# A two-layer decoder trunk on one core: side-by-side products in every later sub-layer, one PSUM pair for the retention's values, paired squares at the start, and no adaLN work in a sub-layer's first three tiles

## The chip, the core and the metric

The kernel runs on one core of a Trainium2 chip. A core has TensorE (PE in the profile, with PEld for its weight loads), VectorE (DVE), ScalarE (ACT), GpSimd (POOL) and SyncE (SP), which here only issues transfers. The metric is the device time of one execution in microseconds (us).

## What is computed

A sequence of 256 positions with 1024 features goes through two layers of three sub-layers each: a SwiGLU feed-forward block (FFN), a mixer (retention in layer 0, a short convolution in layer 1), and a second FFN. Each sub-layer is normalized and modulated by a conditioning vector (adaLN):

```
mod = (silu(c) @ ada_w[l] + ada_b[l])          # shift, scale, gate of the three sub-layers
h = rmsnorm(x, g) * (1 + scale) + shift
x = x + 0.5 * gate * ((silu(h @ w_gate) * (h @ w_up)) @ w_out)      # FFN, 2816 wide
x = x + gate * retention(h)      # q, k, v, g = h @ w_in; 4 heads; (silu(g) * rmsnorm(o)) @ w_out
x = x + gate * short_conv(h)     # b, c, u = h @ w_in; (b * conv3(c * u)) @ w_out
```

All inputs are float32, and the result keeps float32 accuracy.

## The kernel before

Activations lie with 128 features on the partitions and the 256 positions along the row, so x is eight parts x[k]. Every float32 value v is split into two float32r halves, hi and lo = v - hi, and a product of weights W and activations h is the sum of three: W_hi h_hi, W_hi h_lo and W_lo h_hi. `product` issues them for one 128 x 128 weight block in one of two forms. In the *plain* form (lines 287 to 289) there are three matmuls. In the *side-by-side* form (line 285), used where the PSUM region is twice as wide as the operand, one matmul of 512 columns makes W_hi h_hi and W_hi h_lo in two halves of a PSUM bank, and a second (line 289, 256 columns) adds W_lo h_hi to the first half; the halves are added on the way out.

A *tile* of weights is 2048 columns (1 MB, 16 blocks), that is two output blocks of 128 features. `prepare` splits a raw tile: hi by a copy on ScalarE (line 245), lo by a subtraction on VectorE or, for a part of the tiles, on GpSimd (line 250). The pools hold five raw tiles, six hi halves and six lo halves. The list `jobs` fixes the order of the weight tiles; `weights` keeps up to four loaded ahead.

The operand comes in two forms. The *biased* operand `h` is x * scale, split, with the adaLN shift in two further columns (258 in all); it needs no norm, so a sub-layer can begin on it before the norm is known, and `normalized` (line 325) multiplies the product by the reciprocal norm `r` afterwards. The *whole* operand, built by `whole` (lines 433 to 444), is the finished normalized and modulated input: x * r (line 437, alternately VectorE and GpSimd), scale and shift on ScalarE (line 438), the hi copy on ScalarE (line 331) and lo on VectorE (line 332), for each of eight parts, through three rotating buffers `xr`. Before the change only the retention builds it. There the first three tiles (`BIASED`) are plain on the biased operand, and the tiles after them use the whole one: the first of those goes part by part over k and can begin before all parts are there, q and k and v are plain, and the last five gates are side by side, evicted in `projected` by a ScalarE copy of one half (line 312) and a VectorE addition (line 313). The FFNs after the first, and the convolution, run all their input tiles plain on the biased operand. The output projections of all sub-layers are side by side already.

PSUM is four pairs of banks; from the first FFN on, one pair holds the broadcast conditioning vector for good, which leaves three. AdaLN vectors are made by VectorE: a 1 MB tile of `ada_w` is loaded into a raw buffer and reduced by two instructions (line 120). `pace` decides after each weight tile whether a further adaLN tile is loaded (at most one) and reduces the one loaded earlier; it keeps away only from the border between a sub-layer's input and output tiles.

In the retention, step by step, one head's values are projected, then `normalize` of the head before last and `values` of the last one follow: eight matmuls into two pairs of banks, four squares, and a sum of squares by a matmul with ones (line 358). At the program's start the sum of squares of x is eight such matmuls, ahead of everything. Engines run their own instructions in order; a scheduler wrote that order.

## Time and profile before

| what | value |
|---|---|
| median of 3 runs | 1095.13 us (1094.88 to 1095.41) |
| the profiled execution | 1094.71 us, span of its instructions 1092.9 us |
| TensorE busy | 1067.8 us (98% of the span) |
| VectorE, ScalarE, GpSimd busy | 830.8, 578.0, 391.0 us (76%, 53%, 36%) |
| mean granted clock of TensorE | 0.997 of 2.4 GHz |

Matmuls are pipelined, so TensorE's busy time doesn't tell whether it runs at its best: the distance between the starts of matmuls does. About 1.8 us of the time lie around the span.

### The profile page before, as it was taken

The page shows a single profiled execution, that of the slowest core. Times are in us where ns is not written, and L with a number is a line of the kernel's source. Part 1 is how long each engine was busy: PE and PEld are TensorE (multiplying, and loading weights), DVE is VectorE, ACT ScalarE, POOL GpSimd, SP SyncE. Part 2 cuts the span into 40 slices and gives each one's busy share as a digit, 9 for nine tenths or more (in the row PEclk, how much of TensorE's full clock was granted, in tenths as well). Part 3 has the DMA queues.
Part 4 walks back from the last instruction along what each step waited for, and adds up shares of the span by engine and source line. Part 5 has one row for each costly group of instructions (what it writes and reads, how often), then busy time and mean ns, then how long its engine had stood idle before and what let it go on. Part 6 is the DMA issues. An engine that isn't in the chain of part 4 may idle for free.

```text
span 1092.9 us, 19439 instructions
## 1 busy us (share of the span) xinstructions
PE 1067.8 (98%) x7706; PEld 1008.9 (92%) x7706; DVE 830.8 (76%) x1089; ACT 578.0 (53%) x923; POOL 391.0 (36%) x339
## 2 busy tenths in 40 slices
PE   8999999999998999999999999999999989999996
PEld 7999988999887889999988999998899989999985
DVE  6999776998558898887678878767798686666454
ACT  4364444663367655545555644545564484454442
POOL 0034355345354432332445133344411442323352
PEclk9999999999999999999999999999999999999998
DMA  9977779867555687777679767767885545553441
GB/s 344 364 275 275 295 280 314 314 239 296 208 221 198 227 308 274 268 277 261 219 267 324 300 249 297 266 223 264 305 317 210 190 156 191 173 188 123 156 133 39
DMA packets 44573, 268.51 MB, mean 246 GB/s; under 512 B 4801, under 2 KB 6977, under 8 KB 19906
## 3 DMA queue, kind: packets, MB, share of 16 engines
q1 hardware_dynamic: 43138, 266.56, 67.1%
q8 instruction: 60, 0.98, 0.4%
q10 hardware_dynamic: 1344, 0.71, 0.2%
q14 instruction: 31, 0.25, 0.1%
HBM read 266.20 MB, written 1.05 MB: 245 GB/s over the span
## 4 chain that ended last, share of the span: by engine, by line
PE 59%; DVE 2%; issue 0%; ACT 0%; DVEq 0%; ACTq 0%
PE ps L289 20%; PE ps L288 14%; PE ps L287 14%; PE ps L285 11%; DVE lo L250 1%; PE ps L358 0%; DVE rsum L511 0%; DVE h L412 0%; DVE raw L804 0%; DVE r L800 0%; DVE x L514 0%; ACT hi L245 0%; DVEq L877 0%; DVE x L516 0%; ACT std L370 0%
## 5 line engine op out<-in xcount | busy, mean ns | idle before, releaser
L250 DVE TENSOR_TENSOR lo<-raw,hi 128x1024 fp32r<-128x1024 f32 (+1 forms) x300 | 366.6, 1230 | 176.6 <-ACT hi L245 161.1
L245 ACT CAST hi<-raw 128x1024 fp32r<-128x1024 f32 (+2 forms) x408 | 377.7, 937 | 221.2 <-PE ps L288 123.3
L288 PE MATMUL ps<-h,hi 128*128 128x258 f32 (+1 forms) x1520 | 430.4, 283 | 1.7 <-DVE h L412 1.5
L287 PE MATMUL ps<-h,hi 128*128 128x258 f32 (+1 forms) x1520 | 430.5, 283 | 1.1 <-DVE sum L325 1.1
L289 PE MATMUL ps<-h,lo 128*128 128x258 f32 (+1 forms) x1520 | 430.5, 283 | 0.0
L250 POOL TENSOR_TENSOR lo<-raw,hi 128x384 fp32r<-128x384 f32 (+1 forms) x108 | 201.5, 1867 | 290.4 <-ACT hi L245 290.0
L288 PEld LDWEIGHTS ps<-h,hi 128*128 128x128 f32 x1520 | 288.7, 190 | 2.6 <-DVE h L412 1.3
L287 PEld LDWEIGHTS ps<-h,hi 128*128 128x128 f32 x1520 | 289.0, 190 | 1.8 <-ACT sg L586 0.7
L289 PEld LDWEIGHTS ps<-h,lo 128*128 128x128 f32 x1520 | 288.7, 190 | 0.0
L285 PE MATMUL ps<-act,hi 128*128 128x512 f32 x616 | 217.5, 398 | 0.6 <-DVE rsum L511 0.6
L289 PE MATMUL ps<-act,lo 128*128 128x256 f32 x704 | 197.8, 281 | 0.0
L332 POOL TENSOR_TENSOR act<-av,act 128x256 fp32r<-128x256 f32 x88 | 84.0, 957 | 251.2 <-ACT act L331 242.8
L120 DVE CUSTOM_DVE_ANT_0 raw<-raw,ps,misc 128x1024 f32<-128x1024 f32 x124 | 154.5, 1274 | 0.0
L285 PEld LDWEIGHTS ps<-act,hi 128*128 128x128 f32 x616 | 115.6, 188 | 29.4 <-DVE rsum L511 1.7
L289 PEld LDWEIGHTS ps<-act,lo 128*128 128x128 f32 x704 | 133.1, 189 | 0.3 <-DVE lo L250 0.3
L331 ACT CAST act<-av 128x256 fp32r<-128x256 f32 x88 | 35.5, 405 | 100.4 <-DVE av L590 78.3
L325 DVE TENSOR_TENSOR sum<-ps,r 128x516 f32<-128x516 f32 (+1 forms) x103 | 70.7, 690 | 16.1 <-PE ps L289 15.8
L590 DVE SCALAR_TENSOR_TENSOR av<-sum,sg 128x256 f32<-128x256 f32 x66 | 51.9, 786 | 17.8 <-ACT sg L589 17.8
L289 PE MATMUL ps<-whole,lo 128*128 128x256 f32 x208 | 58.5, 281 | 0.0
L589 ACT ACTIVATE sg<-sum 128x256 f32<-128x256 f32 x66 | 33.6, 509 | 26.3 <-DVE sum L325 25.9
L341 ACT ACTIVATE sq<-x 128x256 f32<-128x256 f32 x48 | 19.7, 416 | 51.6 <-DVE x L514 44.3
L348 POOL TENSOR_TENSOR acc<-acc,sq 128x256 f32<-128x256 f32 x32 | 28.0, 875 | 38.8 <-ACT sq L341 33.7
(132 smaller groups left out, 1296.2 us busy)
## 6 DMA issues: line engine op xcount, KB each, us to landing
raw<-in_ffn_in SPq DMA_DIRECT2D x80, 1024.0 KB, 4.9
raw<-in_ada_w SPq DMA_DIRECT2D x64, 1024.0 KB, 5.5
raw<-in_ffn_out SPq DMA_DIRECT2D x64, 704.0 KB, 4.2
raw<-in_ada_w SPq DMA_DIRECT2D x16, 512.0 KB, 6.8
raw<-in_ffn_in SPq DMA_DIRECT2D x16, 512.0 KB, 7.6
raw<-in_ret_g SPq DMA_DIRECT2D x8, 1024.0 KB, 5.1
raw<-in_ret_qk SPq DMA_DIRECT2D x8, 1024.0 KB, 5.1
raw<-in_ret_v SPq DMA_DIRECT2D x8, 1024.0 KB, 4.8
```

The source lines that it names most:

```text
L120: ins = nc.vector.tensor_tensor_reduce(out=w, in0=w, in1=state["cond"], scale=1.0, scalar=misc[:, C_ADAB + 72 * l + col:C_ADAB + 72 * l + ...
L245: nc.scalar.copy(out=hi, in_=raw[:, c:c + m])
L250: eng.tensor_tensor(out=lo, in0=raw, in1=hi, op=ALU.subtract)
L285: nc.tensor.matmul(out=ps, lhsT=hi, rhs=m.rearrange("p n s -> p (n s)"), start=start, stop=False)
L287: nc.tensor.matmul(out=ps, lhsT=hi, rhs=m[:, 0], start=start, stop=False)
L288: nc.tensor.matmul(out=ps, lhsT=hi, rhs=m[:, 1], start=False, stop=False)
L289: nc.tensor.matmul(out=ps[:, :n], lhsT=lo, rhs=m[:, 0], start=False, stop=stop)
L325: nc.vector.tensor_tensor(out=y[:, :, :n], in0=ps[:, :, :n], in1=r[:, :n].unsqueeze(1).to_broadcast([P, 2, n]), op=ALU.mult)
L331: hi = nc.scalar.copy(out=dst[:, 0], in_=src)
L332: lo = eng.tensor_tensor(out=dst[:, 1], in0=src, in1=dst[:, 0].bitcast(F32), op=ALU.subtract)
L589: nc.scalar.activation(out=sg, in_=y[:, 0, :S], func=AF.Silu, bias=y[:, 0, S:S + 1])
L590: nc.vector.scalar_tensor_tensor(out=av, in0=y[:, 1, :S], scalar=y[:, 1, S:S + 1], in1=sg, op0=ALU.add, op1=ALU.mult)
```

## The change

Every sub-layer after the first now builds the whole operand and, after three biased tiles, uses the side-by-side form for its inputs: the three later FFNs (19 of 22 tiles each) and the convolution (9 of 12). For that the pool of 2 KB slots grows from 22 to 30; the conditioning vector moves from a buffer of its own into one of the six of the hi halves, until it is copied to PSUM in the first FFN, and the scaled x of the first sub-layer moves into slots. `values` writes all four blocks of a head into one pair of banks and runs ahead of `normalize`. The squares of x are added in pairs before the sum by matmul. `pace` also does nothing in a sub-layer's first three tiles.

```diff
-    slot_p = ctx.enter_context(tc.tile_pool(name="slot", bufs=22))
+    slot_p = ctx.enter_context(tc.tile_pool(name="slot", bufs=30))
...
-    cond = const.tile([P, D], F32, name="cond")
+    cond = whi_p.tile([P, D], F32, name="cond", tag="hi")
...
-        if any(o - BEFORE <= n < o + BEHIND for o in outputs):
+        if any(o - BEFORE <= n < o + BEHIND for o in outputs) or any(b <= n < b + BIASED for b in begins):
             return
         reduce_loaded()
...
             if f == 1:
+                begins.append(len(jobs))
                 if l % 2 == 0:
...
+            begins.append(len(jobs))
             jobs += [(a["ffn_in"][l, f, b], 2048) for b in range(FB)]
...
-            for i, pair in enumerate(x_pairs):
-                sq = tmp.tile([P, 2, S], F32, name="sq2", tag="rot" if i % 2 else "sum")
-                (nc.gpsimd if i == 1 else nc.vector).tensor_tensor(out=sq, in0=pair, in1=pair, op=ALU.mult)
-                total([sq[:, 0, :], sq[:, 1, :]], ps, i == 0, i == KB // 2 - 1)
+            for i in range(2):
+                sqs = []
+                for j, eng in ((2 * i, nc.vector), (2 * i + 1, nc.gpsimd)):
+                    sq = tmp.tile([P, 2, S], F32, name=f"sq{j}", tag="rot" if i else "sum")
+                    eng.tensor_tensor(out=sq, in0=x_pairs[j], in1=x_pairs[j], op=ALU.mult)
+                    sqs.append(sq)
+                (nc.gpsimd if i else nc.vector).tensor_tensor(out=sqs[0], in0=sqs[0], in1=sqs[1], op=ALU.add)
+                total([sqs[0][:, 0, :], sqs[0][:, 1, :]], ps, i == 0, i == 1)
...
-        for ps in first_projections(h) if n == 0 else [begun]:
-            activate(ps)
+        if n == 0:
+            for ps in first_projections(h):
+                activate(normalized(ps, r, S), None)
+        else:
+            src["whole"] = whole(n, src["r"])
         while len(act) < FB:
-            activate(projections(h))
+            if n:
+                activate(*projected(src))
+            else:
+                activate(normalized(projections(h), r, S), None)
...
             blocks = []
+            ps = banks()
+            for b in range(4):
+                c = slice(b * P, (b + 1) * P)
+                o = ps[:, b // 2, b % 2 * S:(b % 2 + 1) * S]
+                nc.tensor.matmul(out=o, lhsT=v[hd][0][:, c], rhs=sc[:, :S], start=True, stop=False)
+                nc.tensor.matmul(out=o[:, P:], lhsT=v[hd][1][:, c], rhs=sc[:, S:S + P], start=False, stop=True)
             for half in range(2):
-                ps = banks()
...
+            if 0 <= step - 1 < HEADS:
+                raw_o[step - 1] = values(step - 1, sc[step - 1])
             if 0 <= step - 2 < HEADS:
                 o[step - 2] = normalize(step - 2, *raw_o[step - 2])
-            if 0 <= step - 1 < HEADS:
-                raw_o[step - 1] = values(step - 1, sc[step - 1])
...
-    def short_conv(n, h, r, begun):
+    def short_conv(n, src):
         gated = []
+        src["whole"] = whole(n, src["r"])
...
-            taps(d, normalized(projections(h) if d else begun, r), convs[d])
+            taps(*projected(src), convs[d])
```

On TensorE, at the third sub-layer's fourth input tile (its first on the whole operand), two of the eight parts stood as follows before; `h0` and `h1` are parts of the biased operand, `hi` and `lo` the weight halves:

```order
L287 MATMUL ps_4751<-h0_4369,hi_4533 128x258
L288 MATMUL ps_4751<-h0_4369,hi_4533 128x258
L289 MATMUL ps_4751<-h0_4369,lo_4534 128x258
L287 MATMUL ps_4751<-h1_4374,hi_4533 128x258
L288 MATMUL ps_4751<-h1_4374,hi_4533 128x258
L289 MATMUL ps_4751<-h1_4374,lo_4534 128x258
```

And now, one part after the other for both output blocks:

```order
L288 MATMUL ps_4785<-whole_4595,hi_4527 128x512
L292 MATMUL ps_4785<-whole_4595,lo_4528 128x256
L288 MATMUL ps_4785<-whole_4595,hi_4531 128x512
L292 MATMUL ps_4785<-whole_4595,lo_4532 128x256
L288 MATMUL ps_4785<-whole_4601,hi_4527 128x512
L292 MATMUL ps_4785<-whole_4601,lo_4528 128x256
```

Three matmuls of 258 columns became two, of 512 and 256, for each block, and the first such tile needs the parts one by one.

On VectorE, at the start of the same sub-layer, the reciprocal of the norm was followed by this (`ps_986` is the conditioning vector in PSUM, line 120 the adaLN reduction, `av` the FFN's product of gate and up):

```order
L376 RECIPROCAL r_4599<-std_4595 128x256
L250 TENSOR_TENSOR lo_4538<-raw_4531,hi_4537 128x1024
L120 ISA raw_4469,mod1_96<-raw_4469,ps_986,misc_79 128x1024
L120 ISA mod1_96 128x1
L120 ISA raw_4469,mod1_96<-raw_4469,ps_986,misc_79 128x1024
L120 ISA mod1_96 128x1
L325 TENSOR_TENSOR sum_4602<-ps_4530,r_4599 128x2x258
L250 TENSOR_TENSOR lo_4615<-raw_4612,hi_4614 128x1024
L590 SCALAR_TENSOR_TENSOR av_4605<-sum_4602,sg_4604 128x256
```

Now it is followed by this:

```order
L379 RECIPROCAL r_4589<-std_4585 128x256
L253 TENSOR_TENSOR lo_4532<-raw_4525,hi_4531 128x1024
L440 TENSOR_TENSOR xr_4592<-x0_91,r_4589 128x256
L440 TENSOR_TENSOR xr_4604<-x1_92,r_4589 128x256
L328 TENSOR_TENSOR sum_4640<-ps_4524,r_4589 128x2x258
L253 TENSOR_TENSOR lo_4653<-raw_4650,hi_4652 128x1024
L335 TENSOR_TENSOR whole_4595<-xr_4592,whole_4595 128x256
L335 TENSOR_TENSOR whole_4601<-xr_4598,whole_4601 128x256
L335 TENSOR_TENSOR whole_4607<-xr_4604,whole_4607 128x256
L440 TENSOR_TENSOR xr_4616<-x2_93,r_4589 128x256
L594 SCALAR_TENSOR_TENSOR av_4643<-sum_4640,sg_4642 128x256
L328 TENSOR_TENSOR sum_4708<-ps_4649,r_4589 128x2x258
```

The adaLN reductions left this place, and the building of the whole operand came between the weight splits and the evictions.

On TensorE, in the retention's third step, the sum of squares of head 0 (`acc`) stood ahead of the values of head 1 (`sc`, `v`), four matmuls to each of two PSUM tiles (two of each four are shown); the first and the last row belong to the projections of two heads' values:

```order
L658 MATMUL ps_3446<-hi_3348,whole_2547 128x512
L358 MATMUL ps_3523<-acc_3444,ones_82 128x256
L691 MATMUL ps_3534<-sc_3322,v_3414 128x256
L692 MATMUL ps_3534<-sc_3322,v_3416 128x128
...
L691 MATMUL ps_3541<-sc_3322,v_3414 128x256
L692 MATMUL ps_3541<-sc_3322,v_3416 128x128
...
L656 MATMUL ps_3578<-hi_3380,whole_2505 128x512
```

Now the values come first, and all eight (two are shown) go into one PSUM tile:

```order
L668 MATMUL ps_3443<-hi_3346,whole_2543 128x512
L701 MATMUL ps_3520<-sc_3320,v_3412 128x256
L702 MATMUL ps_3520<-sc_3320,v_3414 128x128
...
L361 MATMUL ps_3547<-acc_3441,ones_82 128x256
L666 MATMUL ps_3574<-hi_3378,whole_2501 128x512
```

One PSUM tile less is taken in a step, and the sum of squares moved behind the eight matmuls.

## Rows read from the trace of the kernel before

**Rows 1.** The page of the profiled execution: busy time and instructions of two engines, and the chain of work that ended last by engine.

```profile
PE 1067.8 (98%) x7706; PEld 1008.9 (92%) x7706; DVE 830.8 (76%) x1089; ACT 578.0 (53%) x923; POOL 391.0 (36%) x339
...
PE 59%; DVE 2%; issue 0%; ACT 0%; DVEq 0%; ACTq 0%
```

**Rows 2.** TensorE's `lo` product (line 289) alone, of which there is one for each 128 x 128 weight block, in seven stretches: the input projections of the third, fourth, fifth and sixth sub-layer from their second tile on, then one gate tile of the retention, five output tiles of the retention, and seven half output columns of the fourth sub-layer. Columns: the stretch and its length in us, busy us (instructions that touch the stretch), granted clock (1.00 is 2.4 GHz), DMA share, GB/s. Of the last three counts one instruction began before the stretch.

```profile
419.32:541.58 122.26, 95.76 (x336) 1.00 0.72 267
609.89:732.71 122.82, 95.10 (x336) 1.00 0.71 261
800.99:865.12 64.13, 50.08 (x176) 1.00 0.65 234
897.50:1019.21 121.71, 94.84 (x336) 1.00 0.50 172
356.75:362.30 5.55, 4.43 (x17) 1.00 0.35 106
375.12:402.86 27.74, 22.17 (x81) 1.00 0.71 249
561.68:588.89 27.21, 21.62 (x78) 1.00 0.88 305
```

**Rows 3.** Busy us (instructions) of PE, PEld, DVE, ACT and POOL in the input projections of the third and the sixth sub-layer, in this order after the length.

```profile
419.32:541.58 122.26, 122.26 (x1010) 122.23 (x1009) 97.38 (x123) 62.81 (x95) 39.27 (x34) 1.00 0.72 267
...
897.50:1019.21 121.71, 121.71 (x1011) 121.68 (x1010) 76.19 (x77) 60.32 (x87) 34.38 (x30) 1.00 0.50 172
```

**Rows 4.** Timeline (start us, duration us, engine, line) at the start of the retention: TensorE at its first tile on the whole operand, then VectorE around it.

```profile
228.43 0.28 PE L289 MATMUL ps<-whole,lo 128*128 128x256 f32 x1
229.81 0.39 PE L287 MATMUL ps<-whole,hi 128*128 128x256 f32 x1 [1.10 <-ACT whole L331]
231.10 0.39 PE L288 MATMUL ps<-whole,hi 128*128 128x256 f32 x1 [0.90 <-DVE whole L332]
...
215.19 1.74 DVE L376 RECIPROCAL r<-std 128x256 f32<-128x256 f32 x1
...
222.79 1.27 DVE L120 CUSTOM_DVE_ANT_0 raw<-raw,ps,misc 128x1024 f32<-128x1024 f32 x1
223.99 1.27 DVE L120 CUSTOM_DVE_ANT_0 raw<-raw,ps,misc 128x1024 f32<-128x1024 f32 x1
...
230.63 0.76 DVE L332 TENSOR_TENSOR whole<-xr,whole 128x256 fp32r<-128x256 f32 x2
```

**Rows 5.** Groups of instructions (count, busy us, mean ns of one, idle us before) of VectorE and GpSimd between 205 and 235 us: those that build the whole operand.

```profile
L332 DVE TENSOR_TENSOR whole<-xr,whole 128x256 fp32r<-128x256 f32 x8 | 4.6, 615 | 0.0
L437 DVE TENSOR_TENSOR xr<-x,r 128x256 f32<-128x256 f32 x4 | 2.1, 550 | 0.0
...
L437 POOL TENSOR_TENSOR xr<-x,r 128x256 f32<-128x256 f32 x4 | 4.1, 1030 | 12.1 <-DVE r L376 8.2 <-DVE whole L332 3.9
```

**Rows 6.** Timeline of TensorE in the retention's values, gates and sums of squares; in brackets the idle time before an instruction and what ended it.

```profile
314.92 0.38 PE L692 MATMUL ps<-sc,v 128*128 128x128 f32 x2
316.49 0.70 PE L691 MATMUL ps<-sc,v 128*128 128x256 f32 x2 [1.18 <-ACT std L370]
...
330.33 0.38 PE L692 MATMUL ps<-sc,v 128*128 128x128 f32 x2
331.69 0.70 PE L691 MATMUL ps<-sc,v 128*128 128x256 f32 x2 [0.98 <-ACT std L370]
...
343.78 0.50 PE L285 MATMUL ps<-whole,hi 128*128 128x512 f32 x1 [1.91 <-DVE sum L313]
...
350.67 0.70 PE L358 MATMUL ps<-acc,ones 128*128 128x256 f32 x2 [0.97 <-POOL acc L348]
```

**Rows 7.** Timeline at the start of the third sub-layer: VectorE, then GpSimd; and VectorE at the start of the fifth.

```profile
412.94 0.41 DVE L348 TENSOR_TENSOR acc<-acc,sq 128x256 f32<-128x256 f32 x1
415.52 2.40 DVE L348 TENSOR_TENSOR acc<-acc,sq 128x256 f32<-128x256 f32 x1 [1.38 <-ACT sq L341]
...
421.02 1.75 DVE L376 RECIPROCAL r<-std 128x256 f32<-128x256 f32 x1
...
415.25 2.39 POOL L250 TENSOR_TENSOR lo<-raw,hi 128x1024 fp32r<-128x1024 f32 x1 [6.72 <-ACT hi L245]
...
803.37 1.75 DVE L376 RECIPROCAL r<-std 128x256 f32<-128x256 f32 x1
```

**Rows 8.** Groups of VectorE in the third sub-layer's input projections (420 to 541 us), then of ScalarE and VectorE in the retention's side-by-side gates (340 to 372 us).

```profile
L250 DVE TENSOR_TENSOR lo<-raw,hi 128x1024 fp32r<-128x1024 f32 x35 | 44.9, 1284 | 18.7 <-ACT hi L245 18.7
L120 DVE CUSTOM_DVE_ANT_0 raw<-raw,ps,misc 128x1024 f32<-128x1024 f32 x22 | 27.3, 1277 | 0.0
L325 DVE TENSOR_TENSOR sum<-ps,r 128x516 f32<-128x516 f32 x21 | 14.5, 692 | 2.2 <-PE ps L289 2.2
L590 DVE SCALAR_TENSOR_TENSOR av<-sum,sg 128x256 f32<-128x256 f32 x21 | 13.7, 652 | 4.5 <-ACT sg L589 4.5
...
L312 ACT COPY sum<-ps 128x512 f32<-128x512 f32 x5 | 2.9, 579 | 0.0
...
L313 DVE TENSOR_TENSOR sum<-ps,sum 128x512 f32<-128x512 f32 x5 | 3.3, 669 | 0.0
```

**Rows 9.** Timeline at the program's start: TensorE's sums of squares, and GpSimd's square of one pair of x.

```profile
8.23 4.23 PE L358 MATMUL ps<-sq,ones 128*128 128x256 f32 x12
...
6.36 1.04 POOL L476 TENSOR_TENSOR sq<-x 128x512 f32<-128x512 f32 x1 [5.39 <-DMA x<-in_x]
```

More of the change, by code (lines that the diff above doesn't have):

```diff
@@ L201, in trunk_kernel @@
     outputs = []
+    begins = []
     ready = {}
@@ L483, in first_modulated @@
                 if k % 2 == 0:
-                    pair = tmp.tile([P, 2, S], F32, name=f"xs{k}", bufs=1)
+                    pair = in_halves(slot(F32, "xs"))
                 xs = pair[:, k % 2, :]
@@ L686, in values @@
             blocks = []
-            for half in range(2):
-                ps = banks()
-                for i in range(2):
-                    c = slice((2 * half + i) * P, (2 * half + i + 1) * P)
-                    nc.tensor.matmul(out=ps[:, i, :S], lhsT=v[hd][0][:, c], rhs=sc[:, :S], start=True, stop=False)
-                    nc.tensor.matmul(
-                        out=ps[:, i, P:S], lhsT=v[hd][1][:, c], rhs=sc[:, S:S + P], start=False, stop=True
-                    )
+            ps = banks()
[4 more added lines that the diff above has]
+                nc.tensor.matmul(out=o[:, P:], lhsT=v[hd][1][:, c], rhs=sc[:, S:S + P], start=False, stop=True)
+            for half in range(2):
                 t = slot(F32, "o")
-                nc.scalar.copy(out=t.rearrange("p (n s) -> p n s", s=S), in_=ps[:, :, :S])
+                nc.scalar.copy(out=t, in_=ps[:, half, :])
                 blocks += [t[:, :S], t[:, S:]]
@@ L740, in retention, with taps @@
             output(n, d, [(weights(), 0, gated)])
-    def short_conv(n, h, r, begun):
+    def short_conv(n, src):
         gated = []
-        def taps(d, y, cv):
-            u = tmp.tile([P, S], F32, name="u", tag="sg")
+        src["whole"] = whole(n, src["r"])
+        def taps(y, bias, cv):
             z = tmp.tile([P, S], F32, name="z", tag="av", bufs=3)
-            nc.scalar.activation(out=u, in_=y[:, 1, :S], func=AF.Identity, bias=y[:, 1, S:S + 1])
-            nc.vector.scalar_tensor_tensor(
-                out=z, in0=y[:, 0, :S], scalar=y[:, 0, S:S + 1], in1=u, op0=ALU.add, op1=ALU.mult
-            )
+            if bias is None:
+                nc.vector.tensor_tensor(out=z, in0=y[:, 0, :S], in1=y[:, 1, :S], op=ALU.mult)
+            else:
+                u = tmp.tile([P, S], F32, name="u", tag="sg")
+                nc.scalar.activation(out=u, in_=y[:, 1, :S], func=AF.Identity, bias=bias[1][:, :1])
+                nc.vector.scalar_tensor_tensor(
+                    out=z, in0=y[:, 0, :S], scalar=bias[0][:, :1], in1=u, op0=ALU.add, op1=ALU.mult
+                )
             tap = [misc[:, C_CONV + i * KB + d:C_CONV + i * KB + d + 1] for i in range(3)]
@@ L763, in short_conv @@
             convs.append(pair[:, d % 2 * S:(d % 2 + 1) * S])
-            taps(d, normalized(projections(h) if d else begun, r), convs[d])
+            taps(*projected(src), convs[d])
         for d2 in range(KB // 2):
-            y = normalized(projections(h), r)
+            y, _ = projected(src)
             for i in range(2):
                 yc = y[:, i, :S]
-                nc.vector.scalar_tensor_tensor(
-                    out=yc, in0=yc, scalar=y[:, i, S:S + 1], in1=convs[2 * d2 + i], op0=ALU.add, op1=ALU.mult
-                )
+                nc.vector.tensor_tensor(out=yc, in0=yc, in1=convs[2 * d2 + i], op=ALU.mult)
                 t = in_halves(slot(F32R, "yg"))
```

24 lines of the change are left out of this document (11 added, 13 removed).

## The prediction

> **What bounds the kernel now.** I began with the page: TensorE is busy for 98% of the span, VectorE for 76%, and the chain that ended last is made of TensorE's work and hardly of anything else [rows 1]. So a saving must come from the time that TensorE takes for a weight block, or from one of its few waits. Pipelined matmuls overlap, so I read the first not from busy time but from stretches with a counted number of blocks [rows 2]. There the reader is to see that the same 128 x 128 block has two prices. In the plain form, in the input projections, it is 122.26 us / 336 = 363.9 ns (third sub-layer), 122.82 / 336 = 365.5 (fourth), 64.13 / 176 = 364.4 (fifth), 121.71 / 336 = 362.2 (sixth). In the side-by-side form it is 5.55 us / 16 = 346.8 ns in a gate of the retention, 27.74 / 80 = 346.8 in its outputs, and 27.21 / 77 = 353.4 in an FFN's outputs. The granted clock is 1.00 in all seven, and the plain stretches have no larger wait, so the difference is the form's. The plain form streams 774 columns in three instructions, the other 768 in two: nearly all of the difference goes with the instruction saved.
>
> Then I looked for TensorE's waits that the change touches. At the retention's first tile on the whole operand it waits twice for a part [rows 4]. In the values it waits twice for a PSUM pair that ScalarE's `std` frees, once more before a gate, and once for a sum of squares [rows 6].
>
> **The input projections.** Nineteen of 22 tiles in three FFNs and nine of 12 in the convolution change form, at 16 blocks a tile: 304, 304, 304 and 144 blocks. At 346.8 ns the savings are 304 x 17.1 = 5.2 us, 304 x 18.7 = 5.7, 304 x 15.4 = 4.7 and 144 x 17.6 = 2.5: **18.1 us** in all. With 353.4 ns instead they are 11.1. I take 346.8, because the gates are input tiles of the same width and the same operand; the 353.4 belongs to tiles of 1408 columns. In its section "Wait — 56ns, not 53.3ns?" the Trainium skill's page "TensorE: Matmul & The Clock Gate" has a warm matmul take its columns at 2.4 GHz and some 2.5 ns more. By that a block would fall from 330 to 325 ns, and all 1056 blocks would save an estimated 5.3 us. The trace disagrees with the skill's small fixed cost: its blocks cost 364 and 347 [rows 2].
>
> **Building the operand four times more.** Each new `whole` costs VectorE eight subtractions of 0.615 us and four multiplications of 0.55, 7.1 us, and GpSimd four of 1.03 [rows 5]. That is off TensorE's path as long as the parts arrive in time. In the retention the eighth part was done at 230.63 + 0.76 = 231.4 us, 14.5 us after the reciprocal's end (215.19 + 1.74 = 216.9), and two adaLN reductions (1.27 us each) stood inside this chain [rows 4]. Without them it is 11.9 us. In the third sub-layer the reciprocal ends at 421.02 + 1.75 = 422.8 [rows 7]; the fourth tile begins two tiles after 419.32, at 431.0 [rows 2], and needs the eighth part 14 blocks later, at 435.8. That leaves 13.0 us for 11.9 and a product of gate and up of 0.65 [rows 8]. In the fourth sub-layer the pair of reductions ahead of the reciprocal goes too. In the fifth, 805.1 to 817.5 [rows 2, 7] leaves 12.4 us, and there GpSimd's new order has a low half of 2.39 us [rows 7] ahead of the last part. I take 1.4 us of waiting in the fifth, 0.6 in the other three, **2.0 us** in all. Bounds: nothing, and four times what the retention lost, 4 x 2.4 = 9.7 us.
>
> **The retention.** Its two waits for parts cost 229.81 - 228.43 and 231.10 - 229.81, where 0.12 each is usual: 2.4 us [rows 4]. The two reductions inside the chain go, but GpSimd's low half stays in the middle of it, so I take back **1.7 us** (bounds 0 and 2.4). In the values, from the two matmuls at 314.92 to the next at 316.49 it is 1.57 us, and from 330.33 to 331.69 it is 1.36, where two such matmuls take 0.22: 2.5 us lost to a missing PSUM pair [rows 6]. One pair instead of two, and the sum of squares behind, leaves the third free: **2.5 us** back. The wait of 1.91 us at 343.78 I count at nothing, and this is where a stall goes: the gate after it can start earlier, but the next sum of squares, which waited 0.97 us until 350.67 for GpSimd's additions, is then early by as much. Bounds for all of these waits: 0 and 2.5 + 1.9 + 1.0 = 5.4 us.
>
> **VectorE, catching up.** Evicting a side-by-side tile costs ScalarE 0.579 us more, and VectorE 0.669 instead of 0.692 [rows 8]; ScalarE has half its time free [rows 3]. What `pace` leaves out in three tiles it loads and reduces at one a tile afterwards. Such a tile costs VectorE two low halves, two reductions, a sum and a product: 2.57 + 2.55 + 0.67 + 0.65 = 6.4 us [rows 8], against 5.55 for TensorE [rows 2]. About four in a row put it some 3.6 us behind. The weights split ahead (three tiles) and two PSUM pairs, 11 us, hide that. The cover is thinner than it was: in the third sub-layer VectorE goes from 97.4 of 122.3 us [rows 3] to 104.5 of some 117, 89%. I take **1.0 us** lost; bounds nothing and, if the backlog comes through in the two FFNs with adaLN, 7.
>
> **Start and first FFN.** The paired squares take four of eight matmuls from TensorE (half of the 16 records, of which 12 end 4.23 us after 8.23) and put two operations of about 1.04 us on GpSimd in series behind the last arrival of x [rows 9]: between 1.7 us gained and 2.1 lost, I take nothing, since each side nearly pays for the other. The conditioning vector takes one of six hi halves until the first FFN's eleventh tile: nothing, up to one exposed low half, 1.28 us [rows 8]; I take **0.3**. Larger slots and the moved scaled x cost nothing; the biased operand's bias columns are written earlier and hidden by the 19 tiles that no longer use it.
>
> **Sum.** -18.1 + 2.0 - 1.7 - 2.5 + 1.0 + 0.3 = -19.0 us. Against the profiled execution's 1094.71 us that gives 1075.7. It lies 0.4 under the median of 1095.13, so I forecast **1076.0 us**. Its own range is 1069 to 1081.
>
> **Rivals.** *Dearer pair:* in the FFNs the pair costs 353.4 ns as in their outputs. The sum is then -12.0, 1083 us. For it: the same sub-layers; against it: another tile width. Chance 0.11. *Backlog:* VectorE and GpSimd hold each other up. While GpSimd ran a low half, an addition of 0.41 us on VectorE took 2.40 [rows 7], and 16 new GpSimd multiplications come in where the chain is tight. Parts late by 2.4 us in four sub-layers and a backlog of 7 make -19.0 + 7.7 + 6.0 = -5.3, 1090 us; half of it gives 1083. The Trainium skill's page "SBUF — State Buffer", section "SBUF: two separate sides", calls the two engines' common port pair an exclusive lock held for a whole instruction; the row of 2.40 us agrees. Chance 0.13. *Columns only:* if the saved instruction is worth nothing and only 6 of 774 columns go (0.45 ns each), 1056 blocks save 2.9 us instead of 18.1: 1091 us. Seven stretches speak against it. This is the direction of the Trainium skill's small fixed cost (its TensorE page, above). Chance 0.03. *Slower:* the two-step eviction makes TensorE wait in every tile that carries an adaLN reduction, some 25. The wait of 1.91 us at 343.78 was one, for the addition behind a pair of reductions. It decides from 19.0 / 25 = 0.76 us a tile; at 1.2 us it gives 1106 us. Against it: there the values and a sum of squares held the other pairs, which no FFN has. Chance 0.04. *Not done:* the order still shows a pair of reductions ahead of the reciprocal in the retention and the fifth sub-layer, so the cleared start may bring nothing there: 1078, inside the forecast.
>
> **The numbers.** Forecast 0.69, rivals 0.11, 0.13, 0.03 and 0.04. For 8 in 10 the range takes in the forecast's own and the dearer pair with half of the backlog: 1069 to 1087. A measurement tells 0.2% (2.2 us) from no change. Faster has 0.94, the same 0.02 (a full backlog with a dearer pair), slower 0.04.
>
> **What would show it.** In the changed kernel's profile 1056 blocks fewer should cost three matmuls, and 16-block tiles should follow each other at 5.55 us in the third, fourth and sixth sub-layers (5.65 with the dearer pair). The fourth tile of each should show waits under 1 us for `whole`, that of the fifth 1 to 2. The two waits for `std` in the values should be gone, and the one before the sum of squares at the fourth head should have grown to about 3. VectorE should be near 90% busy in the third and fourth sub-layers. I'm wrong if TensorE waits there for `lo` or for the eviction's addition, or if the tiles keep 5.8 us.

## The result and the profile after

The changed kernel takes 1079.83 us (median of 4 runs, 1078.78 to 1082.49); the kernel before takes 1095.01 beside it. The ratio is 0.986, 95% interval 0.985 to 0.988. That is faster, by 15.2 us where 19.0 were forecast, and inside the range of 1069 to 1087. The profiled execution took 1079.4 us, its span is 1077.6. The same kernel in a second session took 1080.41 (1077.27 to 1081.67).

From the page of the changed kernel: busy time and instructions by engine, and the engines of the chain that ended last.

```profile
PE 1051.5 (98%) x6642; PEld 945.9 (88%) x6642; DVE 845.5 (78%) x1137; ACT 622.0 (58%) x1048; POOL 410.7 (38%) x357
...
PE 57%; DVE 3%; issue 1%; ACT 0%; DVEq 0%; ACTq 0%
```

TensorE has 1064 matmuls fewer than in [rows 1], and it is still what the end hangs on. A table of stretches shows where the 15.3 us between the two profiled executions lie. A stretch reaches from the start of a sub-layer's first matmul on its own operand to that of its first output product, and from there to the next sub-layer's; all are read from the starts of TensorE's matmuls, in us.

| stretch | before | after | forecast | difference |
|---|---|---|---|---|
| start and first FFN, to its outputs | 143.27 | 142.37 | +0.3 | -0.90 |
| retention to its outputs | 161.42 | 160.89 | -4.2 | -0.53 |
| third sub-layer to its outputs | 129.16 | 127.19 | -5.0 | -1.97 |
| fourth | 128.83 | 123.20 | -5.5 | -5.63 |
| fifth | 70.13 | 68.22 | -1.1 | -1.91 |
| sixth | 130.52 | 125.96 | -4.5 | -4.56 |
| all outputs and the end | 329.60 | 329.76 | 0 | +0.16 |

The forecast column is the prediction's own terms put to their stretches; its +1.0 us for VectorE, which had no place, is left out, and the 0.6 us of waiting in three FFNs is shared equally. Two rows miss by over 2 us: the retention and the third sub-layer.

The third first. These are the `lo` products (line 292 now) in five stretches, as in [rows 2]: the first FFN's outputs, the third, fourth, fifth and sixth sub-layer's side-by-side tiles. Behind each length stand TensorE's busy time and count, then those of its weight loads. Of every TensorE count one instruction began before the stretch.

```profile
166.54:189.16 22.62, 17.97 (x65) 12.09 (x64) 1.00 0.88 311
442.82:533.27 90.45, 71.90 (x257) 48.36 (x256) 1.00 0.82 303
618.53:718.37 99.84, 79.78 (x289) 54.08 (x288) 1.00 0.77 286
816.30:849.58 33.28, 26.59 (x97) 18.02 (x96) 1.00 0.73 260
898.57:1003.96 105.39, 85.12 (x305) 57.45 (x304) 1.00 0.52 178
```

A block costs 22.62 / 64 = 353.4 ns, 90.45 / 256 = 353.3, 99.84 / 288 = 346.7, 33.28 / 96 = 346.7 and 105.39 / 304 = 346.7. So the dearer price, which I had put down to tiles of 1408 columns, also stands in the third sub-layer's 2048, but not in the fourth's. Ahead of it stands a stop, TensorE's timeline in the first side-by-side tile:

```profile
433.70 0.28 PE L292 MATMUL ps<-whole,lo 128*128 128x256 f32 x1
434.79 0.50 PE L288 MATMUL ps<-whole,hi 128*128 128x512 f32 x1 [0.80 <-DVE whole L335]
```

The blocks before this stop cost 346.7 ns, those behind it 353.3. The FFN outputs show the same: 346.9 for their first blocks, 353.4 behind a short stop after some 37.

The retention: TensorE's timeline where the fourth head's values and the gates are, and its granted clock behind the second wait.

```profile
338.42 0.50 PE L288 MATMUL ps<-whole,hi 128*128 128x512 f32 x1 [1.60 <-ACT std L373]
...
347.70 0.70 PE L361 MATMUL ps<-acc,ones 128*128 128x256 f32 x2 [3.36 <-POOL acc L351]
...
348.05:352.10 4.05, 4.05 (x15) 3.44 (x14) 3.79 (x4) 2.32 (x4) 1.27 (x1) 0.58 0.01 2
```

Both waits of the values for `std` [rows 6] are gone. The one before the gate is still there, 1.60 us for `std` where it was 1.91 for an eviction. The wait for the sum of squares has grown from 0.97 to 3.36 us, and behind it the granted clock is 0.58 of 2.4 GHz for 4 us, so mostly the level of 1.2: the last three gates, 96 matmuls from 348.05 on, take 18.40 us, where they took 16.83 in the kernel before. What set that sum is seen on ScalarE and then GpSimd:

```profile
337.89 0.47 ACT L373 ACTIVATE std<-ps,eps 128x256 f32<-128x256 f32 x1
340.29 0.20 ACT L334 CAST h<-mod 128x2 fp32r<-128x2 f32 x1 [1.92 <-DVE mod L120]
340.50 1.28 ACT L321 ACT_TABLE_LOAD   x1
341.80 0.72 ACT L321 ACTIVATE gate<-sum 128x256 f32<-128x256 f32 x2
342.43 1.05 ACT L705 COPY o<-ps 128x512 f32<-128x512 f32 x2
343.37 1.04 ACT L344 ACTIVATE sq<-o 128x256 f32<-128x256 f32 x3
...
344.38 1.10 POOL L351 TENSOR_TENSOR acc<-sq 128x256 f32<-128x256 f32 x1
...
346.92 0.72 POOL L351 TENSOR_TENSOR acc<-acc,sq 128x256 f32<-128x256 f32 x1
```

The values' last matmuls began at 336.0 us, but ScalarE copied them out only at 342.43: it stood 1.92 us at a cast that waits for an adaLN reduction, then loaded a table and did the gate.

### The profile page after: what moved, and what is told of

Read it like the earlier page. It is cut to its first block, busy times and chain, and to the rows that moved or that the text cites. A ratio compares the mean times of both kernels' runs of the same rounds, so it can differ in the third digit from the quotient of the medians.

```text
span 1077.6 us, 17508 instructions
## 1 busy us (share of the span) xinstructions
PE 1051.5 (98%) x6642; PEld 945.9 (88%) x6642; DVE 845.5 (78%) x1137; ACT 622.0 (58%) x1048; POOL 410.7 (38%) x357
## 4 chain that ended last, share of the span: by engine, by line
PE 57%; DVE 3%; issue 1%; ACT 0%; DVEq 0%; ACTq 0%
PE ps L288 33%; PE ps L292 19%; PE ps L291 2%; PE ps L290 2%; DVE lo L253 1%; DVE whole L335 0%; DVE rsum L518 0%; PE ps L361 0%; DVE h L415 0%; DVE raw L816 0%; ACT hi L248 0%; DVE xr L440 0%; DVE r L812 0%; DVE sum L328 0%; DVE av L594 0%
## 5 line engine op out<-in xcount | busy, mean ns | idle before, releaser
L253 DVE TENSOR_TENSOR lo<-raw,hi 128x1024 fp32r<-128x1024 f32 (+1 forms) x300 | 370.4, 1244 | 148.9 <-ACT hi L248 138.1
L288 PE MATMUL ps<-whole,hi 128*128 128x512 f32 x1136 | 398.8, 396 | 2.4 <-ACT std L373 1.6
L292 PE MATMUL ps<-whole,lo 128*128 128x256 f32 x1264 | 353.8, 280 | 0.0
L288 PEld LDWEIGHTS ps<-whole,hi 128*128 128x128 f32 x1136 | 213.7, 188 | 53.3 <-ACT std L373 2.0
L292 PEld LDWEIGHTS ps<-whole,lo 128*128 128x128 f32 x1264 | 239.4, 189 | 0.1
L290 PE MATMUL ps<-h,hi 128*128 128x258 f32 (+1 forms) x464 | 131.8, 284 | 1.0 <-DVE sum L328 0.9
L291 PE MATMUL ps<-h,hi 128*128 128x258 f32 (+1 forms) x464 | 131.0, 282 | 1.5 <-DVE h L415 1.4
L292 PE MATMUL ps<-h,lo 128*128 128x258 f32 (+1 forms) x464 | 130.3, 281 | 0.0
L291 PEld LDWEIGHTS ps<-h,hi 128*128 128x128 f32 x464 | 87.9, 190 | 2.5 <-DVE h L415 2.4
L290 PEld LDWEIGHTS ps<-h,hi 128*128 128x128 f32 x464 | 87.6, 189 | 1.5 <-ACT sg L321 1.1
L292 PEld LDWEIGHTS ps<-h,lo 128*128 128x128 f32 x464 | 87.6, 189 | 0.0
L316 DVE TENSOR_TENSOR sum<-ps,sum 128x512 f32<-128x512 f32 x71 | 48.7, 685 | 19.7 <-ACT sum L315 19.7
```

What stands on the lines that cost most here:

```text
L253: eng.tensor_tensor(out=lo, in0=raw, in1=hi, op=ALU.subtract)
L288: nc.tensor.matmul(out=ps, lhsT=hi, rhs=m.rearrange("p n s -> p (n s)"), start=start, stop=False)
L290: nc.tensor.matmul(out=ps, lhsT=hi, rhs=m[:, 0], start=start, stop=False)
L291: nc.tensor.matmul(out=ps, lhsT=hi, rhs=m[:, 1], start=False, stop=False)
L292: nc.tensor.matmul(out=ps[:, :n], lhsT=lo, rhs=m[:, 0], start=False, stop=stop)
L316: nc.vector.tensor_tensor(out=y[:, :, :S], in0=ps[:, :, :S], in1=y[:, :, :S], op=ALU.add)
```

## Experiments

Two questions: what sets the price of a side-by-side block, and what the parts of the change are worth that didn't answer as forecast. Prices below are stretch lengths over counted `lo` products. The two profiled executions of one kernel can begin their first FFN's tiles up to 0.6 us apart (62.14 and 62.71 us), so stretches are compared, and medians beside them.

### The changed kernel again

> The changed kernel once more, nothing edited. Theory A (every stop of TensorE draws the price of the side-by-side blocks anew, 346.7 or 353.5 ns, and it is kept until the next stop): stretches that begin behind a stop (the third sub-layer's tiles from 433.7 us on, the FFN outputs from the fourth half column on, the fifth sub-layer's tiles, the retention's last gates and outputs) may show the other price than in the first profile, stretches with no stop ahead keep theirs from the stretch before, and executions differ by up to some 2 us for each long stretch that is drawn otherwise. Theory B (the price belongs to the program, by its places or its neighbours): all stretches cost the same as in the first profile within 0.2 us. By A also the fall of the granted clock to 1.2 GHz behind the retention's wait of 3.65 us may come or not; it was there in four of the five profiles with this wait so far and not in the one of the fourth sub-layer's earlier operand.

1080.41 us, ratio 0.986 (0.985 to 0.988). The same five stretches in this profile:

```profile
167.04:189.23 22.19, 17.73 (x65) 12.02 (x64) 1.00 0.88 310
442.90:533.36 90.46, 71.90 (x257) 48.36 (x256) 1.00 0.80 303
618.60:718.44 99.84, 79.77 (x289) 54.04 (x288) 1.00 0.77 286
816.53:850.45 33.92, 26.96 (x97) 18.14 (x96) 1.00 0.73 257
899.91:1005.30 105.39, 85.12 (x305) 57.45 (x304) 1.00 0.52 178
```

The first FFN's outputs now cost 22.19 / 64 = 346.7 ns instead of 353.4, and the fifth sub-layer's tiles 33.92 / 96 = 353.3 instead of 346.7, with nothing edited. The fourth and sixth, which have no stop among their side-by-side tiles, are the same to 0.01 us. Theory B is out: the price isn't the program's. Nor is it the chip's alone. Whether these two executions ran on one chip isn't known, but the next four experiments shared one, and the fifth sub-layer's tiles, which none of them edits, cost 353.3, 353.3, 346.7 and 346.7 ns there.

### Everything at another place in SBUF

```
+    slot_p = ctx.enter_context(tc.tile_pool(name="slot", bufs=30))
     wraw_p = ctx.enter_context(tc.tile_pool(name="wraw", bufs=5))
...
-    slot_p = ctx.enter_context(tc.tile_pool(name="slot", bufs=30))
```

> Changed kernel with all data tiles at other places in SBUF: the pool of slots is allocated ahead of the weight pools instead of behind them. The program is otherwise the same. Theory A (history): the same stretches show the same prices, 353.5 ns in the third sub-layer behind its stop, 346.7 in the fourth, fifth and sixth, 353.5 in the FFN outputs from the fourth half column on. Theory B (the place in SBUF): at least one of these stretches changes its price.

1080.68 us in one run. Third sub-layer 353.3, fourth 346.7, fifth 353.3 ns; but the fourth sub-layer's outputs, behind their stop, kept the cheap price (22.19 / 64 = 346.7):

```profile
749.57:771.76 22.19, 17.92 (x65) 12.10 (x64) 1.00 0.84 294
```

Since the price changes without any edit, as shown above, a changed price does not speak for the place. What this adds is the rule that all profiles here keep: side-by-side tiles begin at 346.7 behind plain ones, either price may follow a stop, and outputs go on at the price that their sub-layer's last tiles had.

### The third sub-layer without its stop

```
-        if src["used"] <= BIASED:
+        if src["used"] <= src["biased"]:
...
```

Here `biased` is 4 in the third sub-layer and 3 in all others.

> Changed kernel, but in the third sub-layer alone a fourth tile stays on the operand with the bias columns, so that the whole operand is wanted one tile (5.8 us) later and TensorE should not stop for a part at 433.7 us. Theory A (the price of a side-by-side block depends on what happened before: a short stop of TensorE moves it from 346.7 to 353.5 ns, and it stays there until the next stop): without the stop all 18 side-by-side tiles follow each other at 5.55 us instead of 5.65; the input projections of this sub-layer go from 127.19 us to 127.19 - 0.96 (the stop) - 17 x 0.103 (the tiles) + 0.27 (16 blocks in the plain form) = 124.7, and the first three half columns of its outputs cost 346.7 ns a block too. The profiled execution falls by about 2.7 us. Theory B (the price belongs to the place: this sub-layer's operand, weights or slots): tiles stay at 5.65 us, 126.5 us for the projections, 0.7 less in all. Theory C (VectorE at 84% busy in this sub-layer holds TensorE a little in every tile): tiles stay at 5.65 or get worse.

1078.20 us, ratio 0.984 (0.983 to 0.986). The third sub-layer reaches its outputs in 124.43 us (A: 124.7, B: 126.5). Its 288 side-by-side blocks, and then the fourth sub-layer's outputs ahead of and behind their stop:

```profile
435.95:535.80 99.85, 80.64 (x289) 54.44 (x288) 1.00 0.79 294
721.35:732.44 11.09, 8.96 (x33) 6.05 (x32) 1.00 0.71 240
744.27:766.88 22.61, 17.98 (x65) 12.09 (x64) 1.00 0.87 280
```

No stop, and 346.7 ns throughout: theory A. C falls too, for VectorE has the same work here. Of the 2.8 us won in the stretch the median shows 1.6: in this profile the fifth sub-layer has the dear price (69.12 us instead of 68.22).

### The FFN outputs without their stop

```
-        pss = banks()
+        pss = [banks()[:, 0, :] for _ in range(2)]
...
```

> Changed kernel, but in each FFN's outputs the first two output blocks are accumulated in two PSUM pairs instead of the halves of one, so that the fourth half column need not wait for VectorE to read the first block's sum. Theory A (a stop sets the price of the blocks after it): the stop at about 12.8 us into the outputs goes (0.11 us in the fourth and sixth sub-layers, 0.73 in the first), and the blocks after it stay at 346.7 ns instead of 353.5 in the first, fourth and sixth sub-layers: 62.5 us of outputs become about 61.6 in the fourth and sixth, 63.2 becomes 61.7 in the first, about 3.3 us in all; the third, which comes in at 353.5 already, only loses its stop. Theory B (the price belongs to the place): the stops go, the price stays 353.4 from the fourth half column on, about 1 us in all. Both are wrong if another stop for a PSUM pair takes its place at the start of the outputs.

1075.90 us, ratio 0.982 (0.980 to 0.984). Outputs of the first, fourth and sixth sub-layer, each 128 blocks across the place of the old stop, and last the retention's outputs:

```profile
143.34:187.72 44.38, 35.84 (x129) 24.20 (x128) 1.00 0.87 304
...
720.51:764.89 44.38, 35.85 (x129) 24.19 (x128) 1.00 0.79 276
999.87:1044.25 44.38, 35.85 (x129) 24.19 (x129) 1.00 0.45 147
365.89:405.38 39.49, 31.37 (x113) 21.16 (x112) 1.00 0.74 269
```

The three FFN outputs are all at 346.7 ns: with the stop gone the price stays. The outputs fall from 63.19 to 61.30 us in the first sub-layer, from 62.50 to 61.29 in the third and from 62.30 to 61.29 in the fourth: A, and a little better than its figures. In this profile the third sub-layer's tiles were at 346.7 behind their stop, and the retention's outputs near the dear price, 39.49 / 112 = 352.6, 0.8 us dearer in all than in the first profile of the changed kernel.

### A provoked stop in the fourth sub-layer

The edit is that of the third sub-layer's, with 2 for the fourth and 3 for all others.

> Changed kernel, but in the fourth sub-layer the whole operand is used from the third tile on, one tile (5.7 us) earlier. Its last parts were done at 621.8 us and would be wanted at about 617.6, so TensorE stops there for some 3 to 4 us in all. Theory A (a stop can move the price of the side-by-side blocks): after these stops some stretch of this sub-layer shows 353.5 ns instead of 346.7, up to 17 tiles x 0.10 = 1.8 us. Theory B (the price belongs to the place): all tiles after the stops stay at 5.55 us, as in the changed kernel. If they stay at 5.55 A isn't refuted, since the stops in the retention's gates and in the fifth sub-layer were also followed by 346.7.

1077.88 us in one run. TensorE waited 1.6 us for parts there, where 3 to 4 were expected, and the tiles behind the last stop cost 66.56 / 192 = 346.7 ns. By its text this leaves A standing and tells nothing against B. It gave something else: the retention's wait was the same (3.5 us for `acc`), but this time the clock did not fall. The row is the 4.35 us behind the wait:

```profile
347.65:352.00 4.35, 4.35 (x26) 3.82 (x25) 4.09 (x5) 3.38 (x5) 1.28 (x1) 1.00 0.01 2
```

The 96 matmuls took 16.83 us, so the fall costs 18.40 - 16.83 = 1.57 us where it comes.

### The values as they were

```
-            ps = banks()
-            for b in range(4):
...
             for half in range(2):
+                ps = banks()
...
-            if 0 <= step - 1 < HEADS:
-                raw_o[step - 1] = values(step - 1, sc[step - 1])
             if 0 <= step - 2 < HEADS:
                 o[step - 2] = normalize(step - 2, *raw_o[step - 2])
+            if 0 <= step - 1 < HEADS:
+                raw_o[step - 1] = values(step - 1, sc[step - 1])
```

> Changed kernel with the values as they were: two PSUM pairs, two pairs of matmuls each, and the sum of squares of the head before ahead of them. By the prediction (2.5 us of waiting for the PSUM pairs is worth 2.5 us) the retention is 2.5 us longer than in the changed kernel, 163.4 instead of 160.9. Theory C (what the pairs gave was given back at the fourth head's sum of squares, and the clock's fall besides): the two waits of 1.2 to 1.6 us for ScalarE's deviation come back, the wait at the fourth head goes down from 3.4 to about 1 us and the granted clock stays at 1.00, so that the retention is 159 to 161 us, no longer than with the change or 1 to 2 us shorter.

1078.40 us, ratio 0.985 (0.984 to 0.987). TensorE's timeline in the values of the second and third head, and its granted clock later:

```profile
313.90 0.70 PE L701 MATMUL ps<-sc,v 128*128 128x256 f32 x2 [1.19 <-ACT std L373]
...
329.10 0.70 PE L701 MATMUL ps<-sc,v 128*128 128x256 f32 x2 [0.99 <-ACT std L373]
...
342.20:345.00 2.80, 2.80 (x10) 2.41 (x10) 2.77 (x7) 2.61 (x8) 0.45 (x2) 0.50 0.93 389
```

Both waits are back, and the retention is not longer: 160.27 us against 160.89 and 161.02. There is no wait for the sum of squares at the fourth head any more, but 1.90 us for VectorE's `sum` before a gate, and here it is that wait behind which the clock falls. So theory C is right on the length of the retention and wrong on the clock. The prediction's 2.5 us for this part of the change come out as nothing, or a loss of 0.6 to 0.7; the clock fell in all three profiles.

### No adaLN work among the retention's gates

```
-        if any(o - BEFORE <= n < o + BEHIND for o in outputs) or any(b <= n < b + BIASED for b in begins):
+        if any(o - BEFORE <= n < o + BEHIND for o in outputs) or any(b <= n < b + BIASED for b in begins) or outputs[1] - 5 <= n < outputs[1]:
```

> Changed kernel, but no adaLN job is run in the retention's last five gates either (the two pairs of reductions among the gates move into the retention's outputs and behind). Theory C (TensorE's wait of 3.36 us at 347.7 for the sum of squares of the fourth head is the end of a chain over VectorE, ScalarE and GpSimd in which the pair of reductions at 337.8 stands): the chain is 2.5 us shorter, the wait falls to 1.0 to 1.5 us, TensorE's idle time before it to 1.4 to 1.8, and the granted clock stays at 1.00 behind it: the retention goes from 160.9 to 157 (with the fall gone) or 158.7. Theory D (ScalarE's table loads and GpSimd's own low halves and additions set the time of the sum): the wait stays above 2.5 us. Against C stands what the two pairs do where they go: a wait of TensorE in the retention's outputs or in the third sub-layer's start.

1083.48 us, ratio 0.990 (0.988 to 0.992): 3 us slower than the changed kernel. ScalarE between the third head's values and the fourth's:

```profile
339.03 1.28 ACT L321 ACT_TABLE_LOAD   x1
340.32 0.42 ACT L321 ACTIVATE gate<-sum 128x256 f32<-128x256 f32 x1
340.76 1.28 ACT L373 ACT_TABLE_LOAD   x1
342.05 0.48 ACT L373 ACTIVATE std<-ps,eps 128x256 f32<-128x256 f32 x1
342.55 1.28 ACT L321 ACT_TABLE_LOAD   x1
343.84 0.42 ACT L321 ACTIVATE gate<-sum 128x256 f32<-128x256 f32 x1
344.17 1.06 ACT L705 COPY o<-ps 128x512 f32<-128x512 f32 x2
```

Theory C is refuted as it was stated: without the pair the wait is 3.47 us, no shorter. The pair's 2.5 us went to two more table loads (2.56 us), because the deviation now stands between the two halves of the gate, and the values are copied out no earlier. Theory D's sign is there (a wait above 2.5 us), but with two loads added the run doesn't tell how long the chain would be without the pair and with ScalarE's old order. The moved pairs then delayed the third sub-layer's operand: TensorE stops 1.62 us there, with another fall of the clock behind it.

### adaLN work again in the first three tiles

```
-        if any(o - BEFORE <= n < o + BEHIND for o in outputs) or any(b <= n < b + BIASED for b in begins):
+        if any(o - BEFORE <= n < o + BEHIND for o in outputs):
```

> Changed kernel, but the first three tiles of a sub-layer run adaLN jobs again. By the prediction's rows the two reductions (2.5 us) stand in the chain that builds the whole operand: the retention's wait for its parts grows from 0.98 to 2.4 us, that of the third sub-layer from 0.96 to 2 to 3, in the fourth and fifth 1 to 2.5 us come in; about 5 us in all. The rival: the clearing is worth nothing, since pairs loaded before still stand ahead of the reciprocals, and the waits are the same within 0.5 us.

1087.93 us, ratio 0.994 (0.993 to 0.996): 7.5 us slower than the changed kernel beside it. TensorE's waits for parts of the whole operand (total, times, longest) at the start of the retention, and of the third, fourth and fifth sub-layer:

```profile
PE ps L290 <- ACT whole L334: 1.2, 1, 1.2
PE ps L291 <- DVE whole L335: 0.9, 1, 0.9
...
PE ps L288 <- DVE whole L335: 1.4, 2, 0.8
...
PE ps L288 <- DVE whole L335: 1.6, 3, 0.7
...
PE ps L288 <- DVE whole L335: 2.2, 1, 2.2
```

They sum to 7.3 us, in the changed kernel to 0.7 + 0.8 = 1.5. By stretches the retention is 2.9 us longer than in the second profile of the changed kernel, the fourth sub-layer 4.6 (1.9 of it the dear price behind its new stops: some 288 blocks x 6.6 ns) and the fifth 2.1; the third is 1.2 shorter, since behind its stops it has the cheap price here. So without the cleared start, less than half of the change's gain is left. The rival that it is worth nothing is out.

### The last sum of squares one gate later

```
-            if 0 <= step - 2 < HEADS:
-                o[step - 2] = normalize(step - 2, *raw_o[step - 2])
+            hd = HEADS - 1 if step == HEADS + 2 else step - 2
+            if 0 <= hd < HEADS - 1 or step == HEADS + 2:
+                o[hd] = normalize(hd, *raw_o[hd])
```

> Changed kernel, but the last head's sum of squares and its normalization are put one gate later in the program: TensorE runs a whole gate (5.5 us) between the fourth head's values and the sum that it waited 3.4 us for. Theory E (the wait is only one of order: TensorE's own next work does not need the sum, and the chain over ScalarE, VectorE and GpSimd to it, which moving the adaLN pair did not shorten, can lie beside a gate): the wait of 3.4 us goes, the granted clock stays at 1.00 behind it, and the stretch from the third sub-layer's, that is the retention's, last value projection (327.8 us) to its first output (366.5) falls by 3.4 us, or by 5 against profiles with the fall of the clock; the total by 3.4 to 5. Theory F (ScalarE is behind in this stretch anyway, and the wait comes back at the next eviction or at the first outputs, which need all gated parts): the stretch falls by less than 1.5 us.

1076.10 us, ratio 0.983 (0.981 to 0.984), 3.7 to 4.3 below the changed kernel. TensorE's timeline at the sum, and the stretches ahead of and behind it:

```profile
349.98 0.59 PE L361 MATMUL ps<-acc,ones 128*128 128x256 f32 x2
351.50 0.50 PE L288 MATMUL ps<-whole,hi 128*128 128x512 f32 x1 [0.93 <-DVE sum L316]
...
338.77:350.00 11.23, 11.22 (x65) 9.84 (x66) 8.86 (x14) 8.55 (x16) 6.94 (x8) 1.00 0.49 187
351.50:362.91 11.41, 11.41 (x65) 9.92 (x65) 11.41 (x13) 9.91 (x16) 4.33 (x4) 1.00 0.74 277
```

The sum's matmuls follow the gate without a wait, the clock stays at 1.00, and of the 3.4 us 0.9 comes back as a wait for an eviction. The retention takes 156.98 us instead of 160.89. That is 3.9 us, where E gave 5 against a profile with the fall of the clock and F less than 1.5: theory E, but for the 0.9 that came back.

### All of it together

The fourth tile on the biased operand in the third and fifth sub-layers, two pairs in the FFN outputs, the late sum.

> Changed kernel with what the runs so far point to: the third and fifth sub-layers keep a fourth tile on the operand with the bias columns (no stop at their first tile on the whole operand), the FFN outputs use two PSUM pairs for their first two blocks (no stop there), and the last head's sum of squares one gate later. Sum from the separate profiles: 0.9 us for the stop in the third sub-layer and 0.2 in the fifth, less 0.5 for 32 blocks in the plain form; 0.7 + 3 x 0.1 for the stops in the outputs; where no stop is left the price stays at what the stretch before had, by theory A mostly 346.7 ns, which against the executions with 353.5 gives up to 1.9 us in the third sub-layer, 0.9 in the fifth and 0.8 in each of three outputs; 3.4 to 5 in the retention by theory E, 0 to 1.5 by F. With E about 1070 us, with F about 1074.

1068.41 us (1068.23 to 1070.61), ratio 0.976 (0.975 to 0.977): 11.4 us below the changed kernel and better than E's figure of about 1070. Third sub-layer, fourth's outputs, fifth sub-layer:

```profile
432.87:532.71 99.84, 80.64 (x289) 54.43 (x288) 1.00 0.80 293
717.27:761.65 44.38, 35.85 (x129) 24.20 (x129) 1.00 0.78 276
802.27:846.65 44.38, 35.84 (x129) 24.20 (x129) 1.00 0.63 237
```

The side-by-side tiles of the FFNs and the convolution are at 346.7 ns throughout. The retention keeps two waits, 1.6 us for `std` and 0.7 for an eviction, and behind the first its gates and then its outputs (39.57 / 112) are at 353.3. The retention takes 157.06 us.

## Why the prediction came out as it did

**Columns against instructions: right.** The side-by-side form costs 346.7 ns for 362 to 366, and where no stop comes in between, in the fourth and sixth sub-layers, the forms alone give -5.63 and -4.56 us where 5.7 and 4.7 were forecast. *Columns only* is out.

**What the 353.4 belongs to: wrong.** The step was "the 353.4 belongs to tiles of 1408 columns". It belongs to no tile. A side-by-side stretch has one of two prices, 346.7 or 353.3, and takes it at a stop of TensorE; the same program draws differently in two executions. *Dearer pair*, put at 0.11 for all FFNs together, came true for one of them: in the third sub-layer some 292 blocks behind the stop x 6.6 ns = 1.9 us. (Its sum of -12.0 counts the convolution's 144 blocks too; the FFNs alone give -13.0.) The trace of the kernel before had the evidence. These are the `lo` products (line 289) of the third sub-layer's outputs ahead of their stop, and of the retention's gate tile behind the wait of 1.91 us [rows 6]:

```profile
541.58:552.68 11.10, 8.87 (x33) 1.00 0.69 232
344.11:349.41 5.30, 4.21 (x15) 1.00 0.99 369
```

The outputs begin at 11.10 / 32 = 346.9 ns a block (one of the 33 began before the stretch) and go on at 353.4 behind their stop, with like tiles on both sides. The last row of [rows 2], which is of these same outputs and not of the fourth sub-layer's, lies wholly behind it. The gate, a tile of 2048 columns, costs 5.30 / 15 = 353.3, while the gate in [rows 2] costs 346.8. So the kernel before already spoke against the width of the tile.

**Waits for the new operands: 2.0 forecast, about 1.7 seen.** By the lengths of the side-by-side stretches over their counted blocks it is 1.2 us in the third sub-layer, 0.4 in the fifth, none in the fourth and sixth. The shares were wrong (1.4 was put in the fifth). In the third the chain from the reciprocal's end to the eighth part took 14.3 us (421.34 to 435.60) where 11.9 and a product of 0.65 were reckoned: weight splits, evictions and products of gate and up stand between the parts on VectorE.

**The cleared start: right in sign, its size never worked out.** The text took 1.7 us for it in the retention, where its first tiles on the whole operand fell from 59.51 us to 57.95, and let the pairs count inside the new waits. The run without it is 7.5 us slower. *Not done* is out.

**The values: wrong.** The step was "one pair instead of two [...] leaves the third free: 2.5 us back". The waits went, and the text's own warning came true: it expected the wait before the fourth head's sum to grow to about 3, and it grew to 3.36. What failed is the price: the text set that return against the 1.91 us before the gate alone and let the 2.5 stand. TensorE's early arrival can't be worth more than the chain on ScalarE, VectorE and GpSimd allows, and that chain hardly moved. ScalarE in the kernel before stood at the same cast, just as long, ahead of the same copy:

```profile
343.15 0.19 ACT L331 CAST h<-mod 128x2 fp32r<-128x2 f32 x1 [1.92 <-DVE mod L120]
...
345.29 1.05 ACT L696 COPY o<-ps 128x512 f32<-128x512 f32 x2
```

Counted from the first score matmul (283.75 before, 281.38 now), the fourth head's last value matmul came 3.1 us earlier, this copy 0.5 and the sum of squares 0.6. So 0.6 of the 2.5 us arrived, and the fall of the clock took 1.57. With the old values the retention is no longer. What the chain needs is work of TensorE beside it: a gate put there is worth 3.9.

**VectorE, catching up: 1.0 forecast, none found.** It is 88% busy in the third sub-layer (95.08 of 108.56 us) and 85% in the fourth, near the 90% forecast, and even 96% in the fifth (48.50 of 50.35). The tiles follow each other at 5.55 us in the fourth and at 5.65 in the third, which is the dear price. *Backlog* and *slower* are out: parts came late by 1.7 us in all, and no side-by-side tile of the later FFNs or the convolution waits for an eviction.

**Start and first FFN: 0.3 forecast, -0.90 in one profile, -0.26 in the other.** The two executions of one kernel differ by as much, so nothing can be told.

So of the 3.7 us between the forecast sum of -19.0 and the -15.3 of the profiled executions, the retention cost 3.7 and the third sub-layer 3.0; the start gave 1.2 back, VectorE 1.0 and the fifth sub-layer 0.8. That the total lies so near is in part luck: two misses of 6.7 us together stand against 3.0 us of others the opposite way, of which the start's may be noise.

## What to carry over

A wait is only worth removing at the place where the chain of the other engines ends: before counting it, look for the next wait on the same chain and ask whether that chain starts any earlier; if not, move independent work of the bounding engine in front of the wait. Read a price per block ahead of and behind each short stop, not as a mean of a stretch, and run the same program twice before giving a small price difference to a form or a place. And take the cleared path of a critical chain as a term of its own, worked out with the work put back.

## What the runs showed of the hardware

**Two prices of the same stream.** A pair of a 512-column and a 256-column fp32r product costs 346.7 or 353.3 ns at a granted clock of 1.00. Within a stretch it never changes; behind a stop either may follow. Behind the third sub-layer's stop 1.03, 1.03 and 1.08 us between two starts were followed by 346.7 and 1.08, 1.09, 1.10 and 1.10 by 353.3, but in the fifth, where each of two stops adds 0.19 to 0.25 us to a block, both prices followed without such an order. What decides it stays open; so does why it lasts. Between profiles of different kernels it alone moves a sub-layer's projections by up to 1.9 us (the third's), between the two of the changed kernel by 0.9 (the fifth's). The Trainium skill's page "TensorE: Matmul & The Clock Gate", section "Wait — 56ns, not 53.3ns?", has one fixed cost per warm matmul, about 2.5 ns; by it the pair would be an estimated 325 ns, and no stretch here shows that.

**The fall of the clock is not certain either.** Of eight profiles with a wait of 3.4 to 3.5 us at the fourth head's sum, the granted clock fell towards 1.2 GHz behind it in seven and stayed at 1.00 in one; with the old values it fell behind a wait of 1.90, where the kernel before shows 1.91 [rows 6] and no fall. The Trainium skill's page "TensorE: Matmul & The Clock Gate", section "Part 1: The HAM clock gate", says that the measure of activity runs free of the program, so that the point of change varies; these profiles, in which like waits were followed by a fall or by none, agree.
